# Layer 0's modulations on VectorE, and x's input projections in the context's mixer

## The chip, the core and the metric

The kernel runs on one core of one Trainium2 chip. The metric is the device time of one execution in microseconds (us); lower is better.

## The reference, cut to what matters

One sequence of 256 tokens of width 1024 passes through two blocks. The first block has two layers, each FFN, mixer, FFN (attention in layer 0, an RWKV-7 time mix in layer 1). The second block takes x together with a context of 256 tokens and has two layers; the context is carried through layer 0 only.

```python
# block 1, each layer
x = x + 0.5 * swiglu(rms_norm(x, g0), w_gate0, w_up0, w_down0)
x = x + mixer(rms_norm(x, gm))
x = x + 0.5 * swiglu(rms_norm(x, g1), w_gate1, w_up1, w_down1)
# block 2, each layer l
sh1, sc1, g1, sh2, sc2, g2 = split(silu(c) @ w_mod[l] + b_mod[l], 6)      # w_mod[l]: 1024 x 6144
csh1, ...                  = split(silu(c_ctx) @ w_mod[l] + b_mod[l], 6)
h  = rms_norm(x,  g_norm1) * (1 + sc1)  + sh1
hc = rms_norm(xc, g_norm1) * (1 + csc1) + csh1
glu, gate, q_m, k_m, v_m, q_g, k_g, v_g = sections of h @ w_in[l]         # x, with rope
...                                     = sections of hc @ w_in[l]        # context
x = x + g1 * merge(conv(glu), gate, attention of x over [context, x])
x = x + g2 * conv_ffn(rms_norm(x, g_norm2) * (1 + sc2) + sh2)
if l == 0: xc goes through the same steps, with attention over the context alone
```

So the modulations of a layer are two vectors (c and c_ctx) times one 1024 x 6144 matrix. They depend on no token, and are due when the first norm that uses them is made. The input projection of x in layer 0 needs x after all of block 1, and the layer's first two modulations.

## The kernel before, in words

**Weights.** Every weight matrix lies in DRAM in chunks of 512 KB. `chunk` (L62) loads one by a DMA from SyncE's queue (L68) into `wraw` (four buffers) and splits it: ScalarE makes `whi` (L73), VectorE `wlo = wraw - whi` (L74), three buffers each. Activations are split in the same way (`hhi`, `hlo`), and a product is three matmuls (`mm3` L83, L85 to L87; `mm3T` L149, L151 to L153).

**FFN** (L278, four of them: FFN00 and FFN01 of layer 0, FFN10 and FFN11 of layer 1). The gate/up phase has 11 steps c, each of four chunks. A step's two results are gated on VectorE by four operations of 512 elements (L292, L295, L296, L300). Then come two down phases of 11 chunks each, whose ends update x (L308). After each step `fill` is called.

**Modulations.** A layer's `w_mod` is 48 chunks. They are not split: each chunk is four matmuls (L1283) in which the two columns `csf` (silu of c and c_ctx) are the stationary operand. After each pair of chunks the rows go to DRAM (L1287, L1288), and `adaln_sum` (L1291) later brings them back, adds them in a matmul (L1299) and puts the result, transposed, into `modT`. `adaln(n)` issues n chunks wherever it is called. Before, layer 0's are issued by the FFNs' `fill` at the rates `NF`: 16 in FFN00 (one at each gate/up step, five in the down phase) and eight in FFN01's down phase; the other 24 in the gaps of the RWKV mixer (`gaps`, L1720, where of each step `MODS` is given to modulations and the rest to the context's projections). Layer 1's 48 are all issued in the context's mixer, at the three places of `CM`: between its projections, in its attention, and before `w_out`, with what is left right before its conv-FFN.

**Order of block 2** (`block2`, L1845). First the context's mixer: its layer-0 projections were made early, in block 1, and kept in DRAM, so that `proj` only loads them (`kva`, `gk`, `vg`, `qa`, `gq`), then low-rank norms and products, attention (`attend`: scores L1627, transposes L1634, values L1638), two projections of x (`glu`), the 31-tap convolution on VectorE (L1576), the branch outputs, `w_out`, and the context's conv-FFN. Then x's mixer of layer 0 (starting with the products of `w_in` for groups 0, 1 and 2, 12 chunks), x's conv-FFN, and layer 1.

**What sets the order.** The code is written in program order, and a scheduler then orders each engine's instructions by readiness and buffers; each engine runs its own list in order, and meets the others at semaphores. Loads are issued by SyncE in its own order, as buffers come free.

Of the kernel before, what the change touches and what calls it, by code (L numbers as in the profile page):

```python
# [13 lines left out]
P = 128  # L14
S = 256
# [654 lines left out]
MODS = .16  # L670
# [541 lines left out]
CM = (5,3,8)  # L1212
# [8 lines left out]
class Blk2:  # L1221

    def adaln_prep(s, pa):
# [6 lines left out]
        s.mod_order = [(l, i, hf) for l in range(2) for i in (1, 0, 2, 4, 3, 5) for hf in range(2)]  # L1230
# [60 lines left out]
    def adaln_sum(s, pool, which):  # L1291

        nc = s.nc
        for l, i in which:
# [6 lines left out]
            if i in (2, 5):  # L1301
                ps = s.pt.tile([P, 512], F32, name="tp", tag="tp")
                nc.tensor.transpose(out=ps[:16, :P], in_=m.rearrange("p k c -> p (k c)"), identity=s.ident)
                g = pool.tile([16, P], F32, name="adg", tag="adg", bufs=2)
                nc.scalar.copy(out=g, in_=ps[:16, :P])
                nc.sync.dma_start(out=s.mod[l, i].rearrange("c (k p) -> k c p", p=P), in_=g)
# [141 lines left out]
    def proj_in(s, pool, pv, act, l, rope):  # L1448
# [4 lines left out]
        kept = act is s.actc  # L1453
# [20 lines left out]
    def proj_qa(s, pool, act, l):  # L1474
        A = s.nc.scalar
        qa = pool.tile([P, 2, 416], F32, name="qa", tag="qa")
        if act is s.actc:
            s.nc.sync.dma_start(out=qa, in_=s.kept["in", 1, 0][:, :, :416])
            return qa
# [22 lines left out]
    def proj_gq(s, pool, pq, act, l, rope):  # L1502
        gq = pool.tile([P, 2, 8, 64], F32, name="gq", tag="gq")
        kept = act is s.actc
        if kept:
            s.nc.sync.dma_start(out=gq.rearrange("p t h d -> p t (h d)"), in_=s.kept["in", 2, 0])
# [39 lines left out]
    def glu(s, po, pool, act, l):  # L1546
# [6 lines left out]
        for i in range(2):  # L1553
            if act is s.actc:
                nc.sync.dma_start(out=yf[:, 2 * i:2 * i + 2, 15:15 + S], in_=s.kept["glu", 0, i])
# [109 lines left out]
    def gates(s, po, pool, act, l, branches, gt, halves=(0, 1)):  # L1665

        for br in branches:
            if 0 in halves:
                gt[br] = po.tile([P, 8, S], F32, name=f"gate{br}", tag=f"gate{br}")
            for i in halves:  # L1670
                if act is s.actc:
                    s.nc.sync.dma_start(out=gt[br][:, 4 * i:4 * i + 4], in_=s.kept["gate", br, i])
# [13 lines left out]
    def ctx_steps(s, order):  # L1686
# [5 lines left out]
        for what, br, i in order:  # L1692
# [7 lines left out]
            d = s.kept[what, br, i] = s.kept_pool.tile([P, n, S] if what != "in" else [P, 2, 512], F32, name=f"{what}{br}{i}")  # L1700
# [144 lines left out]
    def block2(s, x, xc, pr, ec, store):  # L1845
# [3 lines left out]
        with s.phase("mixv") as pv, ExitStack() as eo:  # L1849
# [10 lines left out]
            with s.phase("mixp") as pool:  # L1860
                glu = lambda: setattr(s, "yfc", s.glu(pv, pool, s.actc, 0))
# [83 lines left out]
def lay_out(i):  # L1945
# [15 lines left out]
    for l in range(2):  # L1961
        w(f"w_mod{l}", i["w_mod_2"][l], [slice(512 * c, 512 * c + 512) for c in range(12)])
# [19 lines left out]
    a["x"], a["ctx"] = i["x"][0], i["ctx_2"][0]  # L1982
    a["cT"] = np.stack([fm(i["c_2"][0]), fm(i["c_ctx_2"])], 2)
# [30 lines left out]
NF = (1,.6,16),(0,.4,8),(0,0,0),(0,0,0)  # L2014
RC = (9,10)
# [5 lines left out]
class Net(K, Attn, Rwkv, Blk2):  # L2021
    def block1(k, x, pa, late2):
# [4 lines left out]
        with ExitStack() as ea:  # L2027
# [7 lines left out]
            def spread(c, rates):  # L2035

                n = [min(rates[2], int(min(i, 11) * rates[0] + max(i - 11, 0) * rates[1])) for i in (c, c + 1)]
                k.adaln(n[1] - n[0], (k.pa, "at"))

            def early(c):  # L2040
                if c == 0:
                    k.adaln_prep(pa)
                spread(c, NF[0])
                if c == ED:
                    pe = e0.enter_context(k.phase("actc0", "right"))
                    with k.phase("adsum0", "right") as pool:
                        k.adaln_sum(pool, [(0, 0), (0, 1)])
# [5 lines left out]
                        k.csteps = k.ctx_steps(CO)  # L2053
# [78 lines left out]
```

## Time and profile before

| | us |
|---|---|
| median of three runs | 2750.02 |
| lowest and highest of them | 2743.48, 2751.31 |
| the profiled execution | 2742.86 |
| its span, first to last instruction | 2741.2 |
| TensorE busy / VectorE busy / ScalarE busy | 2637.1 / 1939.1 / 1397.1 |
| mean granted TensorE clock, as a share of full speed | 0.975 |

The stages by the trace: FFN00 to 217, attention to 397, FFN01 to 579, FFN10 to 768, the RWKV mixer to about 1145, FFN11 to 1340, the context's mixer to about 1600, its conv-FFN to 1783, then x's layers. A busy share is an average over stages of different limits; the question for each stage is which engine or transfer the others wait for there. Matmuls are pipelined and their ends are modelled, so two matmuls of 0.28 us may start 0.12 us apart, and a busy TensorE is not one at its peak.

### The profile page before, as it was taken

The page shows a single profiled execution, that of the slowest core. Times are in us where ns is not written, and L with a number is a line of the kernel's source. Part 1 is how long each engine was busy: PE and PEld are TensorE (multiplying, and loading weights), DVE is VectorE, ACT ScalarE, POOL GpSimd, SP SyncE. Part 2 cuts the span into 40 slices and gives each one's busy share as a digit, 9 for nine tenths or more (in the row PEclk, how much of TensorE's full clock was granted, in tenths as well). Part 3 has the DMA queues.
Part 4 walks back from the last instruction along what each step waited for, and adds up shares of the span by engine and source line. Part 5 has one row for each costly group of instructions (what it writes and reads, how often), then busy time and mean ns, then how long its engine had stood idle before and what let it go on. Part 6 is the DMA issues. An engine that isn't in the chain of part 4 may idle for free.

```text
span 2741.2 us, 50775 instructions
## 1 busy us (share of the span) xinstructions
PE 2637.1 (96%) x20672; PEld 2287.7 (83%) x20672; DVE 1939.1 (71%) x3166; ACT 1397.1 (51%) x2187; POOL 26.4 (1%) x22
## 2 busy tenths in 40 slices
PE   8999999999989999899898889999999999999999
PEld 8977799889866887799647589888989988889997
DVE  5665676556588544765688568789887856997885
ACT  4455554444445333344564355566566645765563
POOL 0000000000002000000000000000000000000000
PEclk9999999999999999999899889999999999999999
DMA  6675355665543456455565555552345555415554
GB/s 226 217 244 175 123 196 186 208 207 186 188 155 129 155 190 198 135 187 185 189 204 192 190 175 185 171 170 80 117 149 185 182 188 156 128 62 170 171 184 154
DMA packets 148515, 472.31 MB, mean 172 GB/s; under 512 B 22924, under 2 KB 36113, under 8 KB 147769
## 3 DMA queue, kind: packets, MB, share of 16 engines
q1 hardware_dynamic: 148280, 469.07, 52.5%
q8 instruction: 162, 2.65, 0.4%
q14 instruction: 73, 0.59, 0.1%
HBM read 459.43 MB, written 9.57 MB: 171 GB/s over the span
## 4 chain that ended last, share of the span: by engine, by line
PE 86%; DVE 7%; ACT 3%; DMA 2%; issue 1%; SPq 0%; POOL 0%; DVEq 0%; ACTq 0%; POOLq 0%
PE mm L151 9%; PE mm L153 9%; PE mm L152 9%; PE mm L87 8%; PE mm L86 8%; PE mm L85 8%; PE tp L151 6%; PE tp L152 6%; PE tp L153 6%; PE at L1627 2%; PE at L1638 2%; DVE wlo L74 2%; PE tp L1634 2%; PE mm L1283 1%; ACT whi L73 1%
## 5 line engine op out<-in xcount | busy, mean ns | idle before, releaser
L74 DVE TENSOR_TENSOR wlo<-wraw,whi 128x1024 fp32r<-128x1024 f32 (+2 forms) x742 | 898.4, 1212 | 558.1 <-ACT whi L73 546.8
L73 ACT CAST whi<-wraw 128x1024 fp32r<-128x1024 f32 (+2 forms) x742 | 770.5, 1040 | 940.9 <-PE tp L152 301.3
L151 PE MATMUL mm<-hhi,whi 128*128 128x256 f32 x1872 | 537.3, 287 | 10.7 <-ACT whi L73 6.4
L153 PE MATMUL mm<-hhi,wlo 128*128 128x256 f32 x1872 | 532.8, 286 | 4.5 <-DVE wlo L74 4.5
L152 PE MATMUL mm<-hlo,whi 128*128 128x256 f32 x1872 | 533.4, 285 | 0.0
L151 PE MATMUL tp<-hhi,whi 128*128 128x256 f32 x1360 | 388.7, 286 | 0.3
L152 PE MATMUL tp<-hlo,whi 128*128 128x256 f32 x1360 | 383.5, 282 | 0.0
L153 PE MATMUL tp<-hhi,wlo 128*128 128x256 f32 x1360 | 382.9, 282 | 0.0
L151 PEld LDWEIGHTS mm<-hhi,whi 128*128 128x128 f32 x1872 | 358.8, 192 | 19.6 <-ACT whi L73 7.6
L153 PEld LDWEIGHTS mm<-hhi,wlo 128*128 128x128 f32 x1872 | 356.6, 191 | 8.9 <-DVE wlo L74 6.1
L152 PEld LDWEIGHTS mm<-hlo,whi 128*128 128x128 f32 x1872 | 358.6, 192 | 3.9 <-issue 2.5
L151 PEld LDWEIGHTS tp<-hhi,whi 128*128 128x128 f32 x1360 | 257.9, 190 | 4.8 <-issue 2.6
L152 PEld LDWEIGHTS tp<-hlo,whi 128*128 128x128 f32 x1360 | 257.8, 190 | 0.0
L153 PEld LDWEIGHTS tp<-hhi,wlo 128*128 128x128 f32 x1360 | 257.3, 189 | 0.0
L85 PE MATMUL mm<-whi,fh 128*128 128x512 f32 x616 | 244.6, 397 | 0.7 <-ACT fh L1814 0.5
L86 PE MATMUL mm<-wlo,fh 128*128 128x512 f32 x616 | 243.1, 395 | 0.8 <-DVE wlo L74 0.8
L87 PE MATMUL mm<-whi,fl 128*128 128x512 f32 x616 | 243.1, 396 | 0.0
L85 PE MATMUL mm<-whi,hhi 128*128 128x512 f32 (+1 forms) x448 | 182.3, 409 | 7.1 <-ACT hhi L809 4.9
L86 PE MATMUL mm<-wlo,hhi 128*128 128x512 f32 (+1 forms) x448 | 183.1, 409 | 3.3 <-DVE wlo L74 3.1
L87 PE MATMUL mm<-whi,hlo 128*128 128x512 f32 (+1 forms) x448 | 182.1, 408 | 3.5 <-DVE hlo L810 3.5
L1576 DVE SCALAR_TENSOR_TENSOR cy<-yf,cw,cy 128x256 f32<-128x256 f32 x360 | 154.1, 478 | 1.0
L85 PEld LDWEIGHTS mm<-whi,fh 128*128 128x128 f32 x616 | 116.5, 189 | 34.7 <-issue 5.7
(528 smaller groups left out, 3846.1 us busy)
## 6 DMA issues: line engine op xcount, KB each, us to landing
wraw<-in_wgu SPq DMA_DIRECT2D x176, 512.0 KB
wraw<-in_w_up SPq DMA_DIRECT2D x132, 512.0 KB
wraw<-in_w_in SPq DMA_DIRECT2D x124, 512.0 KB
wraw<-in_w_mod SPq DMA_DIRECT2D x96, 512.0 KB
wraw<-in_wd SPq DMA_DIRECT2D x88, 512.0 KB
wraw<-in_w_down SPq DMA_DIRECT2D x66, 512.0 KB
wraw<-in_w_attn SPq DMA_DIRECT2D x24, 512.0 KB
wraw<-in_w_out SPq DMA_DIRECT2D x24, 512.0 KB
```

The source lines that it names most:

```text
L73: a = nc.scalar.copy(out=hi, in_=raw)
L74: v = nc.vector.tensor_tensor(out=lo, in0=raw, in1=hi, op=ALU.subtract)
L85: s.pinned(mm(ps, lhsT=xh, rhs=wh, start=start, stop=False), pin)
L86: mm(ps, lhsT=xh, rhs=wl, start=False, stop=False)
L87: mm(ps, lhsT=xl, rhs=wh, start=False, stop=stop)
L151: s.pinned(mm(ps, lhsT=wh, rhs=xh, start=start, stop=False), pin)
L152: mm(ps, lhsT=wh, rhs=xl, start=False, stop=False)
L153: mm(ps, lhsT=wl, rhs=xh, start=False, stop=stop)
L1576: V.scalar_tensor_tensor(out=y[:, k], in0=yf[:, k, j:j + S], scalar=cw[:, k, j:j + 1], in1=y[:, k], op0=ALU.mult, op1=ALU.add)
L1627: T.matmul(lg[:, j * S:(j + 1) * S], lhsT=q(hs[par])[:, t * P:(t + 1) * P], rhs=k, start=i == 0, stop=i == len(ks) - 1)
L1634: T.transpose(out=tp[:, j], in_=p[:, j * P:(j + 1) * P], identity=s.ident)
L1638: T.matmul(o[64 * par:64 * par + 64, pr], lhsT=kvs[j // 2][1](4 * g + 2 * pr + par, j % 2), rhs=pTs[par][:, j], start=j == 0, stop=j == nt ...
```

## The change

Four parts.

1. **Layer 0's modulations move to VectorE.** `w_mod[0]` is handed over transposed as well (`w_modT0`, 6144 x 1024). Each FFN's `crow` holds silu(c) and silu(c_ctx) in all 128 partitions (1 MB). For each of the 48 tiles of 128 rows, one DMA loads `mraw` (512 KB, two buffers), and two `tensor_tensor_reduce` (L1303 of the changed kernel) multiply it with `crow` and sum over the 1024 elements into one column of `modT`. The first FFN makes `crow` itself (tanh and four VectorE operations) and writes it to DRAM; the two later ones load it from there. The 16 chunks in FFN00, 8 in FFN01 and 24 in the RWKV mixer, with the sums of layer 0, are gone.
2. **The RWKV mixer's gaps** now issue layer 1's modulations, 35 chunks (`MODS` .16 to .2).
3. **The context's mixer** issues the last 13 of layer 1's, all before `w_out`; none between its projections, in its attention, or after `w_out`.
4. **x's five input projections of layer 0** are issued in the context's mixer as `csteps`: the two `glu` groups (8 chunks, which stood behind the attention) between its projections, and groups 0 to 2 (12 chunks, which opened x's mixer) as the filling of its attention. Their results go to DRAM and are loaded where they are used.

The diff, cut:

```diff
-MODS = .16
+MODS = .2
-CM = (5,3,8)
+CM = (6,16)
+XO = [('glu', 0, 0), ('glu', 0, 1)] + [('in', g, 0) for g in range(3)]
...
+    def mod_room(s, pool, first):
...
+        s.crow = pool.tile([P, 2, D], F32, name="crow")
+        if not first:
+            nc.sync.dma_start(out=s.crow, in_=s.silu_d.rearrange("c n -> (c n)").partition_broadcast(P)...)
+            return
+        nc.sync.dma_start(out=s.crow, in_=s.ins["c_rows"].rearrange("c n -> (c n)").partition_broadcast(P)...)
+        for c in range(2):
+            z = s.crow[:, c]
+            t = pool.tile([P, D], F32, name="mjunk", tag="mjunk")
+            A.activation(out=t, in_=z, func=AF.Tanh, scale=0.5)
+            V.scalar_tensor_tensor(out=z, in0=t, scalar=1.0, in1=z, op0=ALU.add, op1=ALU.mult)
+            V.tensor_scalar(out=z, in0=z, scalar1=0.5, scalar2=None, op0=ALU.mult)
+        nc.sync.dma_start(out=s.silu_d..., in_=s.crow[0:1]...)
...
+    def mod_rows(s):
...
+        for i in (1, 0, 2, 4, 3, 5):
+            m = s.modT[:, 0, i]
+            for k in range(8):
+                raw = s.room.tile([P, D], F32, name="mraw", tag="mraw", bufs=2)
+                s.loaded = nc.sync.dma_start(out=raw, in_=s.ins["w_modT0"][(8 * i + k) * P:(8 * i + k + 1) * P])
+                for c in range(2):
+                    t = s.room.tile([P, D], F32, name="mjunk", tag="mjunk")
+                    V.tensor_tensor_reduce(out=t, in0=raw, in1=s.crow[:, c], scale=1.0, scalar=0.0, op0=ALU.mult, op1=ALU.add, accum_out=m[:, k, c:c + 1])
+                if k == 7:
+                    V.tensor_tensor(out=m, in0=m, in1=s.bmodT[:, 0, i, :, None].to_broadcast([P, 8, 2]), op=ALU.add)
...
             if s.turn >= 1:
                 s.turn -= 1
-                s.adaln(s.mods_done < 48, (s.pm, "mm"), pin)
+                s.adaln(1, (s.pm, "mm"), pin)
...
+    def units(s, n):
+        for _ in range(n):
+            next(s.csteps, None)
...
             def between(h):
                 s.gates(pv, pool, s.actc, 0, (1,), gt, h)
-                mods(CM[0])
+                s.ctx_ahead(1)
+            s.act0 = actx
+            s.csteps = s.ctx_steps("x", XO)
...
-                om, og = s.attentions(po, pool, qs, [kvc], lambda: mods(CM[1]))
+                om, og = s.attentions(po, pool, qs, [kvc], lambda: s.units(CM[0]))
                 s.gates(po, pool, s.actc, 0, (2, 0), gt)
+                s.gaps_end()
                 yf = s.glu(pvx, pool, actx, 0)
...
-                s.mix_tail(pool, po, pv, xc, yfc, gt, om, og, 0, 1, lambda: mods(CM[2]))
+                s.mix_tail(pool, po, pv, xc, yfc, gt, om, og, 0, 1, lambda: mods(CM[1]))
...
-NF = (1,.6,16),(0,.4,8),(0,0,0),(0,0,0)
-RC = (9,10)
+NF = (1,.5,16),(.5,.5,16),(.5,.5,16)
...
-            k.ffn(x, st, "wgu01", "wd01", half(st2), lambda c: spread(c, NF[1]))
-            k.ffn(x, st2, "wgu10", "wd10", lambda hf: k.raw_half(raw, x, hf), lambda c: spread(c, NF[2]))
+            with k.phase("mods") as pool:
+                k.ffn(x, st, "wgu01", "wd01", half(st2), spread(pool, NF[1]))
+            with k.phase("mods") as pool:
+                k.ffn(x, st2, "wgu10", "wd10", lambda hf: k.raw_half(raw, x, hf), spread(pool, NF[2]))
```

How the order of the engines changes, at three places. `NF` asks for one tile a step in FFN00 and one every second step in FFN01 and FFN10; the built order has more.

VectorE in FFN00's gate/up phase, before, from one step's first gating operation (`gr`) to the next:

```order
L292 TENSOR_TENSOR gr<-mm,R 128x512
L74 TENSOR_TENSOR wlo<-wraw,whi 128x1024
L295 SCALAR_TENSOR_TENSOR th<-th,gr 128x512
L296 TENSOR_TENSOR th<-th,tp 128x512
L74 TENSOR_TENSOR wlo<-wraw,whi 128x1024
L300 TENSOR_TENSOR fl<-th,fh 128x512
L74 TENSOR_TENSOR wlo<-wraw,whi 128x1024 x2
L292 TENSOR_TENSOR gr<-mm,R 128x512
```

The same in the changed kernel (`mjunk` takes the products that nobody reads, the row after it is the reading of the sum):

```order
L292 TENSOR_TENSOR gr<-mm,R 128x512
L1303 ISA mjunk,modT<-mraw,crow 128x1024
L1303 ISA modT 128x1
L74 TENSOR_TENSOR wlo<-wraw,whi 128x1024
L295 SCALAR_TENSOR_TENSOR th<-th,gr 128x512
L1303 ISA mjunk,modT<-mraw,crow 128x1024
L1303 ISA modT 128x1
L296 TENSOR_TENSOR th<-th,tp 128x512
L74 TENSOR_TENSOR wlo<-wraw,whi 128x1024
L300 TENSOR_TENSOR fl<-th,fh 128x512
L1303 ISA mjunk,modT<-mraw,crow 128x1024
L1303 ISA modT 128x1
```

Such a step has four reductions, two tiles. All 16 tiles of FFN00 stand within its first eight or so steps; of FFN01's the same, within seven and a half; of FFN10's, six stand in FFN01's second down phase and ten in its own first five steps.

TensorE at the beginning of the context's attention, before:

```order
L1283 MATMUL mm<-wraw,csf 2x256 x8
L1627 MATMUL at<-kgT,qgT 128x256 x6
L1283 MATMUL mm<-wraw,csf 2x256 x5
L1627 MATMUL at<-kgT,qgT 128x256 x2
L1283 MATMUL mm<-wraw,csf 2x256 x15
L1428 MATMUL tp<-ident,qm 96x128 x12
```

And a piece of the same attention after it (L1679 and L1686 are the scores and transposes there, L85 to L87 the products of x):

```order
L85 MATMUL mm<-whi,hhi 128x512
L86 MATMUL mm<-wlo,hhi 128x512
L1686 MATMUL tp<-ident,p 128x128 x2
L1679 MATMUL at<-kgT,qgT 128x256
L1686 MATMUL tp<-ident,p 128x128 x2
L1679 MATMUL at<-kgT,qgT 128x256 x3
L87 MATMUL mm<-whi,hlo 128x512
L1690 MATMUL at<-pT,vg 64x256
```

The fillings of the attention are three-pass products with split chunks now, where they were unsplit matmuls of two columns.

TensorE at the start of x's mixer of layer 0, before (end of group 0's product, the transposes of `kva`, group 1's product):

```order
L85 MATMUL mm<-whi,hhi 128x512
L86 MATMUL mm<-wlo,hhi 128x512
L87 MATMUL mm<-whi,hlo 128x512
L1369 MATMUL tp<-ident,kva 128x128 x2
L85 MATMUL mm<-whi,hhi 128x416
L86 MATMUL mm<-wlo,hhi 128x416
```

And after (end of the context's `w_down`, the transposes of `kva`, now loaded, the low-rank product):

```order
L85 MATMUL mm<-whi,fh 128x512
L86 MATMUL mm<-wlo,fh 128x512
L87 MATMUL mm<-whi,fl 128x512
L1418 MATMUL tp<-ident,kva 128x128 x4
L85 MATMUL mm<-whi,lrh 128x512
L86 MATMUL mm<-wlo,lrh 128x512
```

Nothing but the transposes stands between the two products any more.

## Rows read from the trace of the kernel before

**Rows 1.** The page: span, busy time, and the chain that ended last by engine
```profile
span 2741.2 us, 50775 instructions
PE 2637.1 (96%) x20672; PEld 2287.7 (83%) x20672; DVE 1939.1 (71%) x3166; ACT 1397.1 (51%) x2187; POOL 26.4 (1%) x22
PE 86%; DVE 7%; ACT 3%; DMA 2%; issue 1%; SPq 0%; POOL 0%; DVEq 0%; ACTq 0%; POOLq 0%
```
**Rows 2.** Windows: stretch, us, busy by engine (instructions), granted clock, DMA share, GB/s
```profile
27.00:146.00 119.00, 119.00 (x1028) 113.83 (x1027) 75.56 (x85) 52.95 (x63) 0.00 (x0) 1.00 0.66 220
...
397.00:510.00 113.00, 113.00 (x962) 113.00 (x961) 73.56 (x80) 52.81 (x61) 0.00 (x0) 1.00 0.57 188
510.00:580.00 70.00, 70.00 (x353) 52.29 (x352) 35.95 (x39) 29.10 (x37) 0.00 (x0) 1.00 0.67 228
580.00:592.00 12.00, 11.87 (x101) 11.70 (x100) 8.18 (x19) 6.46 (x13) 0.00 (x0) 1.00 0.53 166
...
895.00:1045.00 150.00, 149.64 (x3331) 123.50 (x3330) 74.40 (x125) 52.35 (x86) 0.00 (x0) 0.97 0.53 173
```
**Rows 3.** Windows again: the context's mixer, and the projections that open x's mixer
```profile
1340.00:1382.00 42.00, 31.90 (x192) 22.20 (x193) 35.09 (x111) 29.86 (x65) 0.00 (x0) 0.80 0.65 213
1382.00:1446.00 64.00, 59.86 (x396) 28.11 (x394) 49.33 (x122) 36.92 (x115) 0.00 (x0) 0.95 0.59 199
1446.00:1555.00 109.00, 90.40 (x638) 76.56 (x636) 82.45 (x131) 40.02 (x51) 0.00 (x0) 0.89 0.59 194
1555.00:1600.00 45.00, 35.06 (x184) 26.86 (x185) 20.73 (x46) 16.98 (x36) 0.00 (x0) 0.77 0.48 157
1783.00:1856.00 73.00, 71.16 (x425) 63.10 (x424) 60.73 (x152) 51.16 (x87) 0.00 (x0) 1.00 0.54 164
```
**Rows 4.** VectorE's timeline, FFN00 and FFN01: start, us, line, operation [idle before]
```profile
73.49 0.69 DVE L292 TENSOR_TENSOR gr<-mm,R 128x512 f32<-128x512 f32 x1
...
145.66 0.68 DVE L292 TENSOR_TENSOR gr<-mm,R 128x512 f32<-128x512 f32 x1
...
408.53 0.68 DVE L292 TENSOR_TENSOR gr<-mm,R 128x512 f32<-128x512 f32 x1
410.17 1.23 DVE L74 TENSOR_TENSOR wlo<-wraw,whi 128x1024 fp32r<-128x1024 f32 x1 [0.96 <-ACT whi L73]
411.32 0.68 DVE L295 SCALAR_TENSOR_TENSOR th<-th,gr 128x512 f32<-128x512 f32 x1
...
510.29 0.68 DVE L292 TENSOR_TENSOR gr<-mm,R 128x512 f32<-128x512 f32 x1
```
**Rows 5.** Groups by form, TensorE: the modulations' matmuls, busy, mean ns, idle before
```profile
L1283 PE MATMUL mm<-wraw,csf 128*2 128x256 f32 x544 | 51.8, 396 | 11.2 <-DMA wraw<-in_w_mod 11.1
L1283 PE MATMUL at<-wraw,csf 128*2 128x256 f32 x224 | 18.0, 408 | 0.0
```
**Rows 6.** Groups by form, VectorE and ScalarE: the nearest to a reduction of 1024 elements
```profile
L879 DVE SCALAR_TENSOR_TENSOR k<-m,k 128x1024 f32<-128x1024 f32 x2 | 2.5, 1225 | 0.0
L174 DVE SCALAR_TENSOR_TENSOR rsy<-rst,rsy 128x2 f32<-128x2 f32 x20 | 3.2, 159 | 0.5
L1402 DVE TENSOR_REDUCE qss<-sq 128x16 f32<-128x1024 f32 x3 | 3.6, 1217 | 1.9 <-ACT sq L1400 1.9
L1631 ACT ACTIVATION_READ_ACCUMULATOR p<-at,nm 128x1 f32 x96 | 19.0, 198 | 0.0
```
**Rows 7.** TensorE's timeline, group 0's product of x: its first matmul and the thirtieth
```profile
1783.19 0.40 PE L85 MATMUL mm<-whi,hhi 128*128 128x512 f32 x1
...
1789.97 0.40 PE L87 MATMUL mm<-whi,hlo 128*128 128x512 f32 x1
```
**Rows 8.** Chain of waits in the context's mixer: start us, us, what
```profile
1340.89 6.83 DMA qa<-in
...
1551.66 3.71 DMA wraw<-in_w_mod
...
1592.14 3.22 DMA adz<-part
```

More of the change, by code (lines that the diff above doesn't have):

```diff
@@ L1301, in adaln_sum @@
             if i in (2, 5):
[L1302 to L1306, printed above, removed]
+                s.mod_gate(pool, l, i)
     def modrow(s, pool, l, i, si, name):
@@ L1452, in proj_in @@
         win = f"w_in{l}"
-        kept = act is s.actc
+        d = s.kept_of(act, l, "in", 0, 0)
+        kept = d is not None
         ps = None if kept else s.lin(win, 0, act)
@@ L1476, in proj_qa @@
         qa = pool.tile([P, 2, 416], F32, name="qa", tag="qa")
-        if act is s.actc:
-            s.nc.sync.dma_start(out=qa, in_=s.kept["in", 1, 0][:, :, :416])
+        d = s.kept_of(act, l, "in", 1, 0)
+        if d is not None:
+            s.nc.sync.dma_start(out=qa, in_=d[:, :, :416])
             return qa
@@ L1553, in glu @@
         for i in range(2):
-            if act is s.actc:
-                nc.sync.dma_start(out=yf[:, 2 * i:2 * i + 2, 15:15 + S], in_=s.kept["glu", 0, i])
+            d = s.kept_of(act, l, "glu", 0, i)
+            if d is not None:
+                nc.sync.dma_start(out=yf[:, 2 * i:2 * i + 2, 15:15 + S], in_=d)
                 continue
@@ L1670, in gates @@
             for i in halves:
-                if act is s.actc:
-                    s.nc.sync.dma_start(out=gt[br][:, 4 * i:4 * i + 4], in_=s.kept["gate", br, i])
+                d = s.kept_of(act, l, "gate", br, i)
+                if d is not None:
+                    s.nc.sync.dma_start(out=gt[br][:, 4 * i:4 * i + 4], in_=d)
                     continue
@@ L1684, in ctx_ahead, with kept_of, ctx_steps @@
                 pass
-    def ctx_steps(s, order):
+    def kept_of(s, act, l, *what):
+        return s.kept.get((getattr(act, "who", None), l) + what)
+    def ctx_steps(s, who, order):
         nc = s.nc
@@ L1699, in ctx_steps @@
             n = 4 if what == "gate" else 2
[L1700 removed]
+            d = s.kept[who, 0, what, br, i] = s.kept_pool.tile([P, n, S] if what != "in" else [P, 2, 512], F32, name=f"{what}{who}{br}{i}")
             if what == "in":
@@ L2033, in block1, with spread, step @@
             e0 = ExitStack()
-            def spread(c, rates):
-                n = [min(rates[2], int(min(i, 11) * rates[0] + max(i - 11, 0) * rates[1])) for i in (c, c + 1)]
-                k.adaln(n[1] - n[0], (k.pa, "at"))
+            def spread(pool, rates):
+                def step(c):
+                    if c == 0:
+                        if rates is NF[0]:
+                            k.adaln_prep(pa)
+                        k.mod_room(pool, rates is NF[0])
+                    n = [min(rates[2], int(min(i, 11) * rates[0] + max(i - 11, 0) * rates[1])) for i in (c, c + 1)]
+                    k.mods_rows(n[1] - n[0])
+                return step
             def early(c):
-                if c == 0:
-                    k.adaln_prep(pa)
-                spread(c, NF[0])
+                first(c)
                 if c == ED:
@@ L2052, in early @@
                         k.acts_to_dram(k.act0)
-                        k.csteps = k.ctx_steps(CO)
-            k.ffn(x, st, "wgu00", "wd00", half(st2), early)
+                        k.csteps = k.ctx_steps("c", CO)
+            with k.phase("mods") as pool:
+                first = spread(pool, NF[0])
+                k.ffn(x, st, "wgu00", "wd00", half(st2), early)
             k.attn_prep()
@@ L2067, in block1 @@
             k.rwkv(x, raw, late, lambda hf: k.late_half(k.st, x, hf))
-            def rest(c):
-                spread(c, NF[3])
-                if c == RC[0]:
-                    k.mods_to(48)
-                if c == RC[1]:
-                    with k.phase("adsum", "right") as pool:
-                        k.adaln_sum(pool, [(0, i) for i in range(2, 6)])
             with k.phase("mnorm") as pool:
@@ L2083, in half @@
                     k.mod_half(st[0], x, hf)
-                k.ffn(x, k.st, "wgu11", "wd11", half, rest)
+                k.ffn(x, k.st, "wgu11", "wd11", half)
                 k.actx = st[0].act
+                k.actx.who = "x"
 def program(tc, ins, outs, plans):
```

43 lines of the change are left out of this document (36 added, 7 removed).

## The prediction

> **What bounds the kernel now.** I read the page first: of a span of 2741.2 us TensorE is busy for 96%, and 86% of the chain that ended last is TensorE's [rows 1]. So time taken off TensorE counts where TensorE is full, and nowhere else. The windows by stage tell where that is. In the FFNs' gate/up phases TensorE is busy for 119 of 119 and 113 of 113 us while VectorE has 73.6 to 75.6 [rows 2], and a good two thirds of the RWKV mixer is as full (149.64 of 150) [rows 2]. [...]
>
> The sum is made against the profiled execution, 2742.86 us. The lowest run is 2743.48 and the median 2750.02, so the profile stands 7 us (0.26%) under the median; about 0.3%, or 8 us, is what a measurement of this kernel tells from no change.
>
> **What a modulation costs on TensorE.** Steps of FFN00, with a chunk each, take (145.66 - 73.49) / 6 = 12.03 us, those of FFN01, without, (510.29 - 408.53) / 9 = 11.31 [rows 4]: 0.72 us. The two groups of L1283 give (51.8 + 18.0) / 96 = 0.73 [rows 5]. I take 0.73. The 48 chunks of layer 0 are worth 35 us of TensorE, but those that layer 1 puts into their places in the RWKV mixer are not saved there.
>
> **What a reduction costs on VectorE.** The trace of before has no VectorE operation with a summed output. Below: a two-operand pass over 1024 f32 takes 1.225 us by its record, 1.15 from start to start (410.17 to 411.32) [rows 4, 6], with the reading of the sum free. Above: product and sum as two passes, 1.15 + 1.22 (a tensor reduce of 1024 f32 takes 1217 ns) = 2.4 us [rows 6]. Between them, the pass plus the reading as one more small instruction: the smallest two-operand VectorE operation takes 0.159 us, ScalarE's reading of an accumulator 0.198 [rows 6]. I take 1.15 + 0.15 = 1.30, since the row of the same form and size is the nearest.
>
> [...]
>
> **The FFNs.** A gate/up step has four `wlo` and four gating operations on VectorE, 4 x 1.15 + 4 x 0.69 = 7.36 us [rows 4]. In the changed order a heavy step has four reductions more: 7.36 + 5.2 = 12.56 us. That is above 11.31, so VectorE becomes the bound of heavy steps. `wlo` is three buffers ahead; I count 3.3 us of that lead, a little over a chunk (11.31 / 4 = 2.83), as what an FFN eats before TensorE waits (between 0 and 8.5).
> - FFN00: eight heavy steps 8 x (12.56 - 12.03) = +4.2; three light ones 3 x (11.31 - 12.03) = -2.2; lead -3.3; five chunks less in the down phase -3.7; the first `crow` (1 MB before the next weights on SyncE's queue, four VectorE operations, a write to DRAM that the next loads stand behind) +3. Sum -2.
> - FFN01: 7.5 heavy steps x 1.25 = +9.4, lead -3.3, eight chunks less in a down phase that TensorE fills (70.00 of 70) [rows 2] -5.9. Sum 0.
> - FFN10: five heavy steps +6.2, lead -3.3; its other six tiles stand in FFN01's second down phase (VectorE 35.95 of 70 there, which covers them) and at the hand-over, where VectorE has 8.18 of 12 us already [rows 2]: +2. Sum +5.
> - The loads: a heavy step moves six chunks, 3.1 MB in 12.56 us, 250 GB/s, against 220 in FFN00 now [rows 2]. Costed at nothing; the rival below prices it.
>
> **The RWKV mixer.** 35 chunks in place of 24, in a stage that is full [rows 2]: 11 x 0.73 = +8. Its three parameter loads, which now come later, lie beside matmuls; if that cover went, they would cost a few us once.
>
> **The context's mixer up to `w_out`'s result.** Of layer 1's 48 chunks 42 stand up to there now and six behind it; 13 remain, all before `w_out`. 29 fewer are -21 us of TensorE. In come 12 chunks of x: a matmul of group 0 starts every (1789.97 - 1783.19) / 29 = 0.234 us [rows 7], so 96 x 0.234 + 48 x 0.19 (416 columns) = 31.6 us. Together +10; by counting the whole built order I get +8. By stage: projections +4 (one of x's `glu` groups for ten small chunks). Attention: `glu`'s other group (11.3) and the 31.6 come in, 24 small chunks (17.5) go, so TensorE's 59.9 becomes 85, and VectorE's 49.3 becomes about as much, since the convolution is drawn forward into it: 64 to 90 us, +26. The rest (109 us, TensorE 90.4 of it, part at the lower clock [rows 3]): `glu` leaves (-22.6), the convolution's share leaves, 13 chunks stand in one row before `w_out` and still wait for their loads: about 75 us, -34. I take -8 for denser filling and clock on top of these, in sum -12. Bounds: if idle time and clock losses stay as large as they are, +8; if they shrink to half, -26.
>
> **The tail** (1555 to 1600, TensorE 35.06 of 45, clock 0.77 [rows 3]): six chunks less, whose load (3.71) and whose sums' load (3.22) are on the chain [rows 8]; the sums can be fed earlier: -6, between 0 and -10.
>
> **x's mixer of layer 0.** Groups 0 to 2 are gone from its start: -31.6, in a stretch where TensorE had 71.16 of 73 us [rows 3]. But they hid the loading of `kva` and the low-rank norm, which now stand bare. The context's mixer starts in just that way: `qa` is waited for during 6.83 us [rows 8], and of its first 42 us TensorE idles 10.1, with the clock at 0.80 [rows 3]. So 7 to 18 come back; I take 12, by the idle time and a little clock. Sum -20. What is late next there is VectorE, with 60.73 of 73 us now.
>
> **Sum**: -2 + 0 + 5 + 8 - 12 - 6 - 20 = -27, so 2716 us. The change takes some 40 us of work off TensorE (the order's counts), and gives a third of it back.
>
> **The rivals.**
> - *Reductions as cheap as a plain pass.* At 1.15 a heavy step is 11.96 us, under FFN00's old pace, and the lead covers most of the rest: 20.5 heavy steps have 82 reductions, 82 x 0.15 = -12. If the context's mixer also fills (-26 for -12): 2690. For it: L879 [rows 6]; against: the reading is an instruction of its own in the order.
> - *Loads and buffers.* Two `mraw` buffers, one queue, 250 GB/s. If a reduction with its waits takes 1.6: 82 x 0.3 = +25, 2741. Against: the down phase of FFN01 runs at 228 GB/s with TensorE full [rows 2].
> - *The joined projections bring nothing.* The attention waits for VectorE, whose convolution and splits share a queue with the softmax chain; context and tail 0 (+18), x's start gives back 18 (+6): 2740. For it: VectorE has 82.45 of 109 us behind the attention [rows 3], and dense fillings can be late where small ones were not.
> - *Other side: VectorE overloaded.* At 2.4 us per reduction a heavy step is 17 us and the three gate/up phases run at VectorE's pace: 82 x 1.1 = +90, 2806. It decides against the change from (2758 - 2716) / 82 = 0.51 above my price, 1.8 us. [...]
> - *The change doing less than it says*: the order has no layer-0 chunk left on TensorE, and x's start is bare, so I give this nothing.
>
> **How the numbers follow.** Forecast (2702 to 2733) 0.49; cheap reductions 0.14; loads 0.12; nothing from the projections 0.12; overload 0.08; some other loss, above all a later SyncE queue or a changed clock, 0.05. Range 2680 to 2752: it reaches under the cheap case by its uncertainty and over the two that end at 2740, and leaves out the overload, most of the other losses and a thin lower end. Faster by over 0.3% (under 2742): forecast, cheap case, and a little over half of the two at 2740 with the spread of the runs taken off, 0.71; within 0.3%: 0.13; slower: 0.16.
>
> **What would show it.** The L1303 group at about 1.15 us a reduction and 0.15 a reading; gate/up spacings near 12.6 us in the first eight steps of FFN00 and the first seven of FFN01, 11.3 after that; TensorE waiting for `wlo` in them; the RWKV mixer 8 us longer; the context's attention some 26 longer and what follows some 40 shorter; x's start with 10 us of idle TensorE and a lower clock. A spacing of 11.3 in the heavy steps means that reductions are cheap, one of 17 that they overload VectorE; a context's mixer of unchanged length makes the forecast wrong by its 18 us.

## The result, and the profile after

The changed kernel takes 2715.47 us (median of four runs, 2713.42 to 2729.47), the kernel before 2750.66 (2743.48 to 2755.46): a ratio of 0.9885 with a 95% interval of 0.9845 to 0.9925, so 21 to 43 us faster. The forecast was 2716.0. The total came out as forecast, and most of its terms did not: they missed on both sides. By the medians the gain is 35 us, by the two profiled executions 29.5, where the sum of the forecast had 27.

The page of the profiled execution (2713.42 us), where [rows 1] stand for the kernel before:

```profile
span 2711.7 us, 50106 instructions
PE 2593.8 (96%) x20276; PEld 2272.8 (84%) x20276; DVE 2028.6 (75%) x3336; ACT 1389.4 (51%) x2163; POOL 26.9 (1%) x22
PE 85%; DVE 8%; ACT 3%; DMA 2%; issue 2%; POOL 0%; SPq 0%; DVEq 0%; ACTq 0%; POOLq 0%
```

TensorE is 43 us less busy, VectorE 90 us more, and the span is 29.5 us shorter. To see where, I cut both traces at the same VectorE instructions: the end of each FFN's last update of x, the first gating operation of the next FFN, the updates of the context and of x. The column "again" is a second profile of the unchanged kernel, described below.

| stage, us | before | again | forecast | after |
|---|---|---|---|---|
| start and FFN00 | 217.8 | +0.9 | -2 | -10.2 |
| block 1's attention, to FFN01's first gate | 181.7 | -0.1 | 0 | -6.9 |
| FFN01 | 180.6 | -1.1 | 0 | -5.2 |
| FFN10 with its hand-over | 188.2 | +0.1 | +5 | +0.5 |
| RWKV mixer, to FFN11's first gate | 396.3 | +14.7 | +8 | +23.4 |
| FFN11 | 175.8 | +1.0 | 0 | -0.8 |
| context's mixer to its update | 228.3 | -0.3 | -12 | +5.9 |
| the tail, to the conv-FFN's first update | 86.9 | 0.0 | -6 | -12.9 |
| from the conv-FFN's end to x's first update | 250.4 | +0.2 | -20 | -21.1 |
| all else | 835.1 | -3.0 | 0 | -2.3 |
| sum | 2741.2 | +12.4 | -27 | -29.5 |

**The FFNs.** VectorE's groups by form, and its timeline in one heavy step of FFN00 (start, us, line, operation):

```profile
L1303 DVE CUSTOM_DVE_ANT_0 mjunk<-mraw,crow 128x1024 f32<-128x1024 f32 x96 | 116.8, 1216 | 2.2 <-DMA mraw<-in_w_modT 1.9
L1303 DVE DVE_READ_ACCUMULATOR2_ANT modT<- 128x1 f32 x96 | 7.7, 80 | 0.0
```
```profile
51.88 0.08 DVE L1303 DVE_READ_ACCUMULATOR2_ANT modT<- 128x1 f32 x1
51.88 0.68 DVE L292 TENSOR_TENSOR gr<-mm,R 128x512 f32<-128x512 f32 x1
52.49 2.35 DVE L74 TENSOR_TENSOR wlo<-wraw,whi 128x1024 fp32r<-128x1024 f32 x2
54.76 0.68 DVE L295 SCALAR_TENSOR_TENSOR th<-th,gr 128x512 f32<-128x512 f32 x1
55.36 1.22 DVE L1303 CUSTOM_DVE_ANT_0 mjunk<-mraw,crow 128x1024 f32<-128x1024 f32 x1
56.50 0.08 DVE L1303 DVE_READ_ACCUMULATOR2_ANT modT<- 128x1 f32 x1
56.50 0.68 DVE L296 TENSOR_TENSOR th<-th,tp 128x512 f32<-128x512 f32 x1
...
63.40 0.68 DVE L292 TENSOR_TENSOR gr<-mm,R 128x512 f32<-128x512 f32 x1
```

A reduction has the record of a plain two-operand pass (1216 ns against 1225 in [rows 6]); the reading of the sum starts at the same instant as the operation behind it (51.88, 56.50) and costs nothing. No idle time stands in the step. It takes 63.40 - 51.88 = 11.52 us, which is eight passes of 1.14 and four gating operations of 0.60 from start to start. So the lower bound of the reduction's price holds, and the gating operations were taken 0.09 too long as well: their record of 0.68 overlaps with what comes next. On VectorE a heavy step is 0.2 us above TensorE's 11.31, not 1.25.

That 0.2 us does not reach TensorE. Its matmuls that open a step (here two of FFN00, five steps apart, all while VectorE's steps are heavy), and all that it waits for from 25 to 150 us:

```profile
51.17 0.28 PE L151 MATMUL mm<-hhi,whi 128*128 128x256 f32 x1
...
107.70 0.28 PE L151 MATMUL mm<-hhi,whi 128*128 128x256 f32 x1
```
```profile
PE mm L153 <- DVE wlo L74: 2.7, 1, 2.7
PE tp L151 <- ACT R L324: 0.2, 1, 0.2
```

TensorE's steps are (107.70 - 51.17) / 5 = 11.31 us, as long as steps without any reduction [rows 4]; it waits for VectorE's `wlo` once, in the second step. In FFN01's gate/up phase it waits for nothing. VectorE falls behind by 0.2 us a heavy step, the split chunks that lie ready cover that, and it catches up in the light steps, which take it 10.4 to 10.5 us. So TensorE still sets the pace of these steps, and what FFN00 gains there is its own chunk: 11.31 for 12.03.

**The context's mixer.** Windows by stage (projections; attention; to the context's update; tail), and what TensorE waits for between 1500 and 1575 (in total, times, longest):

```profile
1341.00:1382.00 41.00, 31.71 (x186) 27.10 (x185) 36.75 (x110) 29.31 (x61) 0.00 (x0) 0.83 0.49 154
1382.00:1474.00 92.00, 88.94 (x497) 66.87 (x497) 83.35 (x174) 58.20 (x138) 0.00 (x0) 1.00 0.53 161
1474.00:1575.00 101.00, 77.97 (x510) 61.04 (x506) 61.71 (x92) 34.34 (x46) 0.00 (x0) 0.83 0.50 169
1575.00:1649.00 74.00, 68.93 (x478) 63.99 (x479) 57.27 (x98) 41.94 (x67) 0.00 (x0) 0.95 0.51 160
```
```profile
PE mm L1336 <- DMA wraw<-in_w_mod: 12.8, 8, 3.6
PE mm L151 <- ACT cvh L1655: 6.7, 1, 6.7
PE mm L85 <- ACT whi L73: 2.4, 1, 2.4
```

The attention became 24 us longer (92.8 against 68.4 by the first score and the last value product), as forecast: TensorE 89 and VectorE 83 of 92 us. The stretch behind it became only 18 shorter (100.8 against 118.9), where 34 was forecast. In it TensorE waits 12.8 us for loads of the 13 modulation chunks (L1336) and 6.7 us for the convolution, and its granted clock is 0.83. The projections took 40.6 us instead of 41.0, where +4 was forecast. SyncE's timeline, and what SyncE itself waits for between 1495 and 1550, tell why those loads are late:

```profile
1499.57 4.62 SPq L68 DMA_DIRECT2D wraw<-in_w_mod  x3
...
1507.72 2.36 SPq L1341 DMA_DIRECT2D part<-junk  x3
1518.58 7.54 SPq L68 DMA_DIRECT2D wraw<-in_w_mod  x3
1527.76 1.87 SPq L1341 DMA_DIRECT2D part<-junk  x4
```
```profile
SPq L1341 <- ACT junk L1340: 12.9, 4, 5.7
SPq L68 <- DVE wlo L74: 12.8, 4, 8.5
```

Between 1510 and 1518 no load goes out: of the four chunks asked for by then one has been used (at 1503), and the matmuls of the others stand in TensorE's order behind the convolution's product, which starts at 1510.5. SyncE waits there for 8.5 us until a weight chunk is split and its buffer free. Then the chunks come one by one, and the writes of finished rows (`part`), for which SyncE waits 12.9 us in all, stand between the loads. That this is the cause is my reading here; the run with the chunks elsewhere tests what the row costs, not each of these waits.

**x's start.** TensorE waits 5.0 us for `kva`, and the clock falls to a mean of 0.84:

```profile
PE tp L1418 <- DMA kva<-inx: 5.0, 1, 5.0
```
```profile
1778.00:1800.00 22.00, 16.55 (x88) 13.39 (x88) 16.87 (x72) 15.90 (x36) 0.00 (x0) 0.84 0.39 131
```

5.5 us idle and 0.16 x 22 = 3.5 of clock make 9, and 31.6 - 21.1 = 10.5 came back. The forecast had 12.

### The profile page after: what moved, and what is told of

It reads as the page before. It is cut to its first block, busy times and chain, and to the rows that moved or that the text cites. A ratio compares the mean times of both kernels' runs of the same rounds, so it can differ in the third digit from the quotient of the medians.

```text
span 2711.7 us, 50106 instructions
## 1 busy us (share of the span) xinstructions
PE 2593.8 (96%) x20276; PEld 2272.8 (84%) x20276; DVE 2028.6 (75%) x3336; ACT 1389.4 (51%) x2163; POOL 26.9 (1%) x22
## 4 chain that ended last, share of the span: by engine, by line
PE 85%; DVE 8%; ACT 3%; DMA 2%; issue 2%; POOL 0%; SPq 0%; DVEq 0%; ACTq 0%; POOLq 0%
PE mm L153 9%; PE mm L152 9%; PE mm L151 9%; PE mm L87 8%; PE mm L86 8%; PE mm L85 8%; PE tp L151 6%; PE tp L152 6%; PE tp L153 6%; PE at L1679 2%; PE at L1690 2%; DVE wlo L74 2%; PE tp L1686 1%; ACT whi L73 1%; PE mm L1336 1%
## 5 line engine op out<-in xcount | busy, mean ns | idle before, releaser
L74 DVE TENSOR_TENSOR wlo<-wraw,whi 128x1024 fp32r<-128x1024 f32 (+1 forms) x742 | 896.8, 1210 | 441.3 <-ACT whi L73 432.1
L73 ACT CAST whi<-wraw 128x1024 fp32r<-128x1024 f32 (+1 forms) x742 | 770.3, 1040 | 889.3 <-PE mm L87 309.5
L153 PEld LDWEIGHTS mm<-hhi,wlo 128*128 128x128 f32 x1872 | 355.0, 190 | 13.1 <-DVE wlo L74 10.2
L85 PE MATMUL mm<-whi,fh 128*128 128x512 f32 x616 | 243.3, 395 | 0.7 <-ACT fh L1875 0.5
L87 PE MATMUL mm<-whi,fl 128*128 128x512 f32 x616 | 242.8, 395 | 0.0
L85 PE MATMUL mm<-whi,hhi 128*128 128x512 f32 (+1 forms) x448 | 180.5, 405 | 7.2 <-ACT hhi L809 4.8
L86 PE MATMUL mm<-wlo,hhi 128*128 128x512 f32 (+1 forms) x448 | 181.7, 406 | 3.7 <-DVE wlo L74 3.5
L87 PE MATMUL mm<-whi,hlo 128*128 128x512 f32 (+1 forms) x448 | 181.0, 405 | 3.5 <-DVE hlo L810 3.5
L85 PEld LDWEIGHTS mm<-whi,fh 128*128 128x128 f32 x616 | 116.5, 189 | 29.3 <-ACT fh L1875 1.7
```

The lines of the kernel that those rows point to most:

```text
L73: a = nc.scalar.copy(out=hi, in_=raw)
L74: v = nc.vector.tensor_tensor(out=lo, in0=raw, in1=hi, op=ALU.subtract)
L85: s.pinned(mm(ps, lhsT=xh, rhs=wh, start=start, stop=False), pin)
L86: mm(ps, lhsT=xh, rhs=wl, start=False, stop=False)
L87: mm(ps, lhsT=xl, rhs=wh, start=False, stop=stop)
L153: mm(ps, lhsT=wl, rhs=xh, start=False, stop=stop)
```

## The experiments

### How much one execution differs from another

A second profile of the unchanged kernel, and RWKV's stage with fewer chunks (below).

> The kernel before, a second profile. In the first one the granted clock fell to half for some 12 us at the start of block 1's attention (227 to 240 us); in the changed kernel it didn't, and the attention is 6.9 us shorter although no instruction of it changed. Theory A (the fall belongs to this kernel: it comes with what stands ahead of it): it is there again at the same place, FFN00's end to FFN01's first gate 181 to 182 us. Theory B (an accident of one execution): it is absent or elsewhere, 175 us.

It took 2755.25 us. The fall of the clock is there again at the same place. Windows of the kernel before (the first 24 us of the attention, three of them by themselves; the RWKV mixer), then the same of the second profile, and of the changed kernel:

```profile
218.00:242.00 24.00, 24.00 (x84) 16.80 (x84) 9.79 (x32) 9.39 (x25) 0.00 (x0) 0.72 0.46 150
230.00:233.00 3.00, 3.00 (x8) 1.92 (x6) 1.03 (x1) 0.10 (x1) 0.00 (x0) 0.50 0.32 83
768.00:1165.00 397.00, 372.73 (x5288) 293.06 (x5288) 256.57 (x425) 156.68 (x240) 20.89 (x8) 0.96 0.48 159
```
```profile
219.00:243.00 24.00, 24.00 (x84) 16.76 (x83) 9.71 (x32) 9.39 (x24) 0.00 (x0) 0.72 0.47 151
768.00:1179.00 411.00, 378.21 (x5283) 296.28 (x5284) 257.46 (x424) 156.71 (x240) 21.36 (x8) 0.94 0.47 153
```
```profile
208.00:232.00 24.00, 24.00 (x114) 17.48 (x113) 12.58 (x34) 12.94 (x29) 0.00 (x0) 1.00 0.56 176
747.00:1166.00 419.00, 388.24 (x5369) 297.49 (x5368) 259.00 (x427) 157.67 (x244) 21.37 (x8) 0.95 0.51 167
```

By itself that spoke for theory A, but the kernels below show that the fall is not tied to this kernel. In three of them the clock falls there too, and the attention is 1.0 to 1.1 us shorter than in the kernel before: the one without the join, whose built order of TensorE is word for word that of the changed kernel until behind FFN11 (mean clock of the attention's first 30 us 0.83), the doubled one (0.77), and the one with 16 tiles in FFN11 (0.83). In two (24 chunks, chunks in the attention) it doesn't (1.00), and they are 6.9 us shorter, like the changed kernel. Of the three with all modulations on VectorE two have 1.00 in these 30 us, and are 5.2 us shorter; the third, with 27 tiles in FFN00, is 0.1 us shorter, which fits a fall of the clock. So of the 6.9 us the fall is 5.8, which an execution has or hasn't; the 1.0 that is left stands in each of the kernels that follow with 16 tiles to an FFN. In the kernel before the granted clock goes from 1.00 (222 to 226) to 0.50 (228 to 241) for some 13 us while TensorE is busy without a break (24.00 of 24 us), with the products of `w_attn` and the bias's small ones between them. What decides it stays open.

The RWKV mixer is worse: the same kernel took 396.3 us there in one profile and 410.9 in the other, with 372.73 and 378.21 us of busy TensorE and a clock of 0.96 and 0.94. The first profile of the kernel before, on which the prediction was made, is the shorter of the two. Against the second, the changed kernel's 419.7 are +8.8, where +8 was forecast.

### What a chunk costs in the RWKV mixer

```diff
-MODS = .2
+MODS = .16
-                s.adaln(1, (s.pm, "mm"), pin)
+                s.adaln(s.mods_done < 24, (s.pm, "mm"), pin)
```

> The changed kernel with 24 instead of 35 of layer 1's chunks in the RWKV mixer's gaps; the other 11 join the row before w_out. Theory A (a chunk in the RWKV mixer costs 2 us: 0.73 of TensorE, the rest idle time and lost clock): RWKV mixer 18 to 23 us shorter, back to the length it had before. Theory B (a chunk costs 0.73; the other 15 us come from loads that stand later): RWKV mixer 8 us shorter. Under both the row before w_out becomes longer by 11 chunks at the pace of loads, 2.5 us each, 27 us: total 2722 under A, 2734 under B.

2723.05 us (ratio to the kernel before 0.9905, 0.9875 to 0.9935). The RWKV mixer took 406.3 us, 13.4 less than in the changed kernel: between the theories. With the runs that follow there are 35 chunks in four profiles (418.2 to 424.8, mean 420.9), 32 in one (414.9), 24 in three (396.3, 410.9, 406.3, mean 404.5), none in three (395.8, 395.9, 388.8, mean 393.5). From none to 35 that is 27 us, 0.78 a chunk, and near the price of 0.73. From 24 to 35 alone it is 16 us by the means, 1.5 a chunk, with 15 us between the three profiles with 24; so the price of these 11 chunks stays open, and the 2 us that one profile gave are not shown. Of the 24 chunks left for the context, 16 stand in the row and eight behind `w_out`; its mixer and tail became 18.6 us longer by the 11 chunks, 1.7 each where 2.5 was expected, more than twice the 0.78; 11.8 us of that stand in the tail, with the eight.

### The join alone

```diff
-XO = [('glu', 0, 0), ('glu', 0, 1)] + [('in', g, 0) for g in range(3)]
+XO = []
```

> The changed kernel with x's five layer-0 projections put back: the two glu groups behind the context's attention, groups 0 to 2 at the start of x's mixer. The 13 modulation chunks stay in one row before w_out. Theory A (the join only moves work: 31.6 us of TensorE leave x's mixer and enter a context's attention that was already near full on TensorE and VectorE, so it is worth 0 to 5 us by itself, and the context's mixer gains from the chunks that are gone): x's mixer 20 us longer, the context's mixer 15 to 20 us shorter, total 2716 to 2722. Theory B (the join is where the gain of the change lies, since the context's mixer has idle TensorE): x's mixer 20 longer, the context's mixer at most 5 shorter, total about 2732.

2735.31 us (0.9935, 0.9911 to 0.9958). Without the join x's start is as long as before (250.4), the context's mixer 10.1 us shorter than with it and its tail 3.5 longer. So the join is worth 21.1 + 3.5 - 10.1 = 14 us, or 11 without the tail, which is 3.5 longer in the doubled kernel too, where the join is in. Theory A's 0 to 5 are refuted; the context's mixer is between the theories, and the total is 3 us above theory B's. (The medians are 20 us apart; the profiles also differ by the clock's fall at the attention, 5.8, and by 5.1 in the RWKV mixer.) The windows (attention; to the update) and the waits in the latter show what the moved products fill:

```profile
1388.00:1455.00 67.00, 65.43 (x432) 50.61 (x431) 59.46 (x128) 46.22 (x122) 0.00 (x0) 1.00 0.32 111
1455.00:1574.00 119.00, 81.03 (x507) 62.94 (x505) 77.40 (x130) 34.30 (x47) 0.00 (x0) 0.80 0.44 143
```
```profile
PE mm L151 <- ACT cvh L1655: 12.0, 1, 12.0
PE mm L1336 <- DMA wraw<-in_w_mod: 10.8, 7, 3.3
PE tp L1638 <- DVE cy L1628: 7.8, 1, 7.8
```

Without x's products in it the attention is 67 us, and the 120 convolution operations on VectorE aren't done when it ends: TensorE waits 12.0 + 7.8 us for them. With the products the attention is 25 us longer, and VectorE uses them for the convolution. I had booked that time as a cost of the attention, and too little of it as a gain behind it.

### The row of chunks before `w_out`

```diff
+            filled = []
+            def fill():
+                filled.append(1)
+                s.units(CM[0]) if len(filled) <= 3 else mods(3)
-                om, og = s.attentions(po, pool, qs, [kvc], lambda: s.units(CM[0]))
+                om, og = s.attentions(po, pool, qs, [kvc], fill)
```

> The changed kernel with the 13 chunks issued three at a time in the later part of the context's attention (behind x's projections) instead of in one row before w_out. Theory A (in the row each chunk waits for its load while SyncE has nothing else to send early; the idle time and the lower clock that it brings are pure loss): the row's 16 us of waits go, attention becomes 5 to 10 longer, total 2700 to 2708. Theory B (what ends the stretch is the chain of the convolution, which takes the place of the waits): within 4 us of the changed kernel.

2698.54 us (0.9808, 0.9773 to 0.9842): theory A for the total, a little below its range. The attention didn't become longer, as theory A had it: it took 90.4 us, 2.4 less than with the row, and the stretch behind it 84.0 instead of 100.8. The chunks also pushed 43 of the 144 matmuls of x's groups, some 10 us, out of the attention into that stretch, so it is the whole context's mixer, 18.5 us shorter, that counts. The stretch's window, and what TensorE still waits for there:

```profile
1471.00:1555.00 84.00, 76.17 (x461) 67.33 (x457) 67.50 (x96) 37.12 (x45) 0.00 (x0) 0.94 0.54 173
```
```profile
PE mm L151 <- ACT cvh L1655: 7.1, 1, 7.1
```

TensorE idles 7.8 us here, 7.1 of them in the wait for the convolution, so that the modulations' loads have 0.7 of it at most where they had 12.8, and the clock is back from 0.83 to 0.94; that wait stays. So the row cost 17 us by the medians, 18.5 by the stage.

### No chunks in the context's mixer at all

```diff
-        s.mod_order = [(1, i, hf) for i in (1, 0, 2, 4, 3, 5) for hf in range(2)]
+        s.mod_order = [(1, i, hf) for i in (2, 4, 3, 5) for hf in range(2)]
...
-        for i in (1, 0, 2, 4, 3, 5):
+        for l, i in [(0, i) for i in (1, 0, 2, 4, 3, 5)] + [(1, 1), (1, 0)]:
...
-                k.ffn(x, k.st, "wgu11", "wd11", half)
+                k.ffn(x, k.st, "wgu11", "wd11", half, spread(rows, NF[3]))
```

> The changed kernel with 16 tiles of layer 1's modulations made on VectorE in FFN11 as well (two of its six modulations); the 32 chunks that remain go to the RWKV mixer and none to the context's mixer. Theory A (the row before w_out cost its waits, its matmuls and the clock): the context's mixer up to the first update of the context 22 to 28 us shorter, FFN11 2 to 4 longer, total about 2692. Theory B (another chain fills the stretch, the convolution's or the loads of w_out): context's mixer 10 shorter, total about 2706.

2676.33 us (0.9729, 0.9701 to 0.9757). The context's mixer is 39.7 us shorter than in the changed kernel, more than theory A's 22 to 28, and FFN11 is not longer. The stretch behind the attention is 62.6 us, with TensorE full and the clock at 1.00:

```profile
1474.00:1537.00 63.00, 62.00 (x407) 55.96 (x404) 50.54 (x67) 31.61 (x40) 0.00 (x0) 1.00 0.52 164
```

In this built order 60 of the convolution's 120 operations stand in FFN11 already, where VectorE has time (in the changed kernel it is busy for 104.92 of 175 us there, from 1166 to 1341), and no wait for the convolution is left. That wasn't intended; the scheduler found the room. It is the likely source of the surplus: in the last experiment below that wait goes too, and the context's mixer becomes 8.7 us shorter with the same 96 tiles. A run that moves the convolution alone was not made. Work also moved from the attention (73.8 us for 92.8) to the projections (58.0 for 40.6); the two together are only 1.6 us shorter, so the gain lies in the stretch.

### VectorE with twice the reductions

```diff
-                for c in range(2):
+                for c in (0, 0, 1, 1):
```

> The changed kernel with each reduction done twice (the second writes the same sum to the same place): 192 instead of 96, no more loads. Theory A (VectorE becomes the bound of a heavy step at once): a heavy step goes from 11.5 to 7.36 + 8 x 1.15 = 16.6 us; with some 20 of them the three FFNs become about 100 us longer, total 2810. Theory B (the tiles spread over more steps, since a third of VectorE's time in an FFN is free): 96 x 1.15 = 110 us more of VectorE go into its free time, about 70 us of 180 per FFN of which 37 are used: FFNs 15 to 40 us longer in sum, total 2735 to 2755.

2730.42 us (0.9925, 0.9905 to 0.9946), 15 more than the changed kernel: theory B's mechanism, a little below its lower edge of 2735. Groups by form and FFN00's second and last gate:

```profile
L1303 DVE CUSTOM_DVE_ANT_0 mjunk<-mraw,crow 128x1024 f32<-128x1024 f32 x192 | 233.7, 1217 | 1.9 <-DMA mraw<-in_w_modT 1.1
```
```profile
45.44 0.68 DVE L292 TENSOR_TENSOR gr<-mm,R 128x512 f32<-128x512 f32 x1
...
148.42 0.68 DVE L292 TENSOR_TENSOR gr<-mm,R 128x512 f32<-128x512 f32 x1
```

117 us more of VectorE made FFN00 11 us longer, of which 6 stand in its first step (which takes eight reductions), FFN01 0.5 and FFN10 1.5, together 13.4; of what else its profile is longer, 5.8 us are the clock's fall at the attention and 3.5 the tail. The scheduler keeps four reductions to most steps ((148.42 - 45.44) / 9 = 11.44 us) and lets the others go on into the down phase. In that gate/up phase TensorE waits for `wlo` once again, 5.6 us. So the rival "VectorE overloaded" was priced wrongly: the load doesn't pile up in the heavy steps.

### All modulations on VectorE

The two last changes together: all 96 tiles, 24 in each FFN, `MODS = 0`, `s.mod_order = []`, and the sums of layer 1 gone.

```diff
-NF = (1,.5,16),(.5,.5,16),(.5,.5,16)
+NF = (1.6,.4,24),(1.5,.4,24),(1.5,.4,24),(1.5,.4,24)
```

> All 96 tiles of both layers on VectorE, 24 in each of the four FFNs, no modulation on TensorE. Theory A (TensorE bounds the FFNs and the RWKV mixer, and VectorE and the loads still have room): context's mixer 25 shorter, RWKV mixer 23 to 40 shorter, FFNs 2 to 5 us longer each: total 2655 to 2680. Theory B (two reductions beside each chunk overload VectorE or the loads: six chunks a step are already near 265 GB/s): each FFN 10 to 15 longer, total 2700 to 2715. Theory C (the RWKV mixer lives on fillings, and without the chunks its gaps are bare): RWKV mixer no shorter, total about 2700.

2659.15 us (2656.11 to 2664.29; 0.9669, 0.9649 to 0.9689): theory A, and the best version of the study, 56 us faster than the changed kernel by the medians. Each FFN is as long as with 16 tiles, within 3 us. The RWKV mixer is 24 shorter. The context's mixer is 28 shorter, but 12 longer than with 16 tiles in FFN11: none of the convolution stands in FFN11, and TensorE waits for it again.

```profile
PE mm L151 <- ACT cvh L1655: 8.6, 1, 8.6
```

Two other shares of the tiles were meant to save that wait: 27, 30, 31 and 8, and 24, 28, 28 and 16.

> All 96 tiles on VectorE as in the run with all rows, but 27, 30, 31 and 8 in the four FFNs instead of 24 each, so that VectorE is freer in FFN11 and a part of the context's convolution (13 of its 120 operations by the built order) comes into FFN11. Theory A (with all rows the wait of 8.6 us for the convolution's result in the context's mixer is VectorE's missing time in FFN11; the three earlier FFNs have VectorE time left): that wait becomes 3 to 6 us shorter, FFN01 and FFN10 at most 3 longer, total 2653 to 2660. Theory B (30 tiles overload VectorE in FFN01 and FFN10): each 6 to 10 us longer, total 2668 to 2675.

> All 96 tiles on VectorE, 24, 28, 28 and 16 in the four FFNs; by the built order none of the convolution comes into FFN11. Theory A (only the convolution's place counts): the context's mixer as with 24 each, total within 5 us of it, about 2659. Theory B (the load on VectorE in FFN11 counts by itself): FFN11 2 to 3 us shorter, context's mixer 5 shorter, total 2652.

2666.5 us (0.9705, 0.9679 to 0.9732) and 2666.28 (0.9706, 0.9682 to 0.973). With 8 tiles in FFN11 the wait for the convolution went whole, where theory A had 3 to 6 us of its 8.6, and the context's mixer became 8.7 us shorter; but FFN01 and FFN10 together became 6 longer and FFN00 2, so nothing was won, and the total lies above theory A's range. With 16 the context's mixer is the same to 0.1 us and FFN11 is no shorter, as theory A has it, and FFN00 and FFN01 are 9 longer, 5 of them in FFN00, which has the same 24 tiles; what made it longer stays open. No verdict in the total between these and the equal share: the intervals overlap.

## Why the prediction was right, and where it was not

1. **FFNs: too dear by 18 us.** Forecast +3 together, measured -15. The step that failed is "so VectorE becomes the bound of heavy steps". Its price went wrong first: "I take 1.15 + 0.15 = 1.30" for a reduction, and with it "4 x 0.69" for the gating operations. In a full VectorE only the distances from start to start count: 1.14 and 0.60, and the reading is free, so a heavy step is 11.52 and not 12.56. With 0.2 us above 11.31 the lead, which the forecast did have, covers all of it, and TensorE keeps its 11.31. At that pace FFN00's eight heavy steps are -5.8 where +4.2 less the lead was forecast, and those of FFN01 and FFN10 cost next to nothing: their gate/up phases are 0.7 and 0.2 us longer than before. (FFN10's own phase has 12 reductions in the trace, three heavy steps' worth and not the five of the forecast; the other 20 stand ahead of it.) The gains of the down phases without chunks, -5.7 and -6.0 (-3.7 and -5.9 forecast), show TensorE's part, which was right.
2. **Block 1's attention: not a term, -6.9.** Of this 5.8 is a fall of the clock that an execution has or hasn't; three kernels whose code there is the changed one's have it.
3. **RWKV mixer: +8 forecast, +23.4 measured against the profile used, +8.8 against a second one.** What failed is taking one profile's stage as that stage's length; its spread of 15 us is larger than the term. The price of a chunk, 0.73, fits the line from none to 35 chunks (0.78), but for the step from 24 to 35 the runs leave it open (1.5 by the means).
4. **Context's mixer: -12 forecast, +5.9 measured.** Attention +26 was right (+24.4), projections +4 came to -0.4. The term that failed is "about 75 us, -34" for the stretch behind, with the -8 on top: measured -18. I named the row of 13 chunks and its loads, and took too little for it. It cost 17 to 18.5 us, as the run with the chunks in the attention shows; the wait of 6.7 us for the convolution had no term at all.
5. **Tail: -6 forecast, -12.9 measured.** The window of before, to hold against the last one of the context's windows above:

```profile
1568.00:1655.00 87.00, 77.42 (x526) 68.48 (x524) 61.62 (x104) 46.08 (x74) 0.00 (x0) 0.88 0.56 178
```

   TensorE is 8.5 us less busy, where the four chunks in this window are some 3 us of matmuls, idles 4.5 less, and its clock is 0.95 instead of 0.88. How the rest divides between the clock and the sums' loads isn't shown, and two other kernels with the same tail (the doubled one and the one without the join) took 77.5 us there instead of 74.0.
6. **x's start: -20 forecast, -21.1 measured**, with the returned time at 10.5 of the 12 I took. The row for it, the context's own start [rows 3, 8], was a good likeness.
7. **The rivals.** "Reductions as cheap as a plain pass" was the truth on VectorE, and its 2690 would have needed a context's mixer that fills; the runs without the row show that it could. "The joined projections bring nothing" is refuted (11 to 14 us). "VectorE overloaded" assumed 2.4 us for a reduction; the trace has 1216 ns with the accumulator, and 1225 for a pass of the same size without [rows 6]. It names the reduction CUSTOM_DVE_ANT_0 and the pass SCALAR_TENSOR_TENSOR, so what a SCALAR_TENSOR_TENSOR with an accumulator takes is not shown.

The total was right because the errors cancelled, and that is luck: 18 us too pessimistic in the FFNs, 7 in the attention and 7 in the tail, against 15 and 18 too optimistic in the RWKV and the context's mixer. The stage table, not the total, is what a forecast should be held against.

## What to carry to other kernels

Work that is independent of the tokens and stands on the bounding engine belongs to the engine with idle time in the same stage. Its cost on that engine is the distance from start to start in a packed stretch, not the record's length (here 1.14 us for 1.216), and what it costs the kernel is read from the bounding engine's own spacing: here 11.31 us with and without reductions. Small weight chunks in one row can cost more than their matmuls: 13 in a row before `w_out` cost 17 to 18.5 us more than the same 13 spread through an attention. Before a term of a few us is read from a stage, that stage should be seen in two profiles of the same kernel.

## What the runs showed of the hardware that was not expected

- The reading of VectorE's accumulated sum takes 80 ns by its record and starts together with the next operation; it adds nothing to the distance of 1.14 us.
- The granted clock falls to half (0.50) for some 13 us at the start of block 1's attention in some profiles and not in others, also between two kernels whose TensorE instructions stand in the same order up to there (the changed one and the one without the join): 5.8 us between these two.
- The RWKV mixer's length differs by 15 us between two profiles of one kernel, with 5.5 us more of busy TensorE, 8.5 more of idle time, and a clock of 0.94 for 0.96.
